# Centring a head's values as they are turned, before the recurrence, instead of centring its outputs

## The chip, the cores and the metric

One core of one Trainium2 chip. The metric is the device time of one execution in microseconds (us); lower is better. A core has a matrix engine (TensorE, PE in the rows, with its weight loads as PEld), a vector engine (VectorE, DVE), a scalar engine (ScalarE, ACT), GpSimd (POOL) and a queue that issues the transfers (SyncE, SP). PSUM is the memory into which TensorE writes, in banks of 128 x 512 float32.

## What is computed

A decoder trunk of two layers on one sequence of 512 tokens of width 1024. Every layer is a half-weighted SwiGLU block, a mixer, and another half-weighted SwiGLU block, each behind an RMS norm and added to the state. The mixer of layer 0 is an RWKV-7 recurrence over 12 heads of 64 channels, beside an attention to a memory of 256 tokens; that of layer 1 is a dilated window attention, beside the same kind of memory attention. What matters here is how the recurrence's output is normalized:

```
def step(state, inp):
    r_t, w_t, k_t, v_t, kk_t, a_t = inp
    sa = einsum('bhvk,bhk->bhv', state, -kk_t)
    state = state * w_t + sa[..., None] * (kk_t * a_t) + v_t[..., None] * k_t
    return state, einsum('bhvk,bhk->bhv', state, r_t)

y = rwkv7_scan(r_h, w_h, k_h, v_h, kk, a_h)
mean = jnp.mean(y, axis=-1, keepdims=True)
var = jnp.mean(jnp.square(y - mean), axis=-1, keepdims=True)
y = (y - mean) * lax.rsqrt(var + LNX_EPS) * lnx_g + lnx_b
bonus = jnp.sum(r_h * k_h * r_k, axis=-1, keepdims=True) * v_h
y = (y + bonus) * g
```

The state is linear in v, row by row of its v index, and so is the output. The mean of y over a head's 64 channels is therefore what the recurrence gives for the mean of v over these channels; with values whose mean over a head is zero, y has mean zero.

## The kernel before

Activations lie as channels x tokens: tiles of 128 channels and all 512 tokens. A dense product splits both operands in a high and a low float32r part and adds three matmuls of 128x512 (`dense`); ScalarE makes a weight tile's high part (`whi`), VectorE or GpSimd the low one (`wlo`), and SP fetches the weights (`raw`). Small products, those of the recurrence among them, are plain float32.

The mixer of layer 0 (`mixer_a`) works on 6 pairs of heads, 128 channels each, and in chunks of 64 tokens. For each pair:
- `projections` makes k, r and v with dense products.
- `rwkv_prepare` makes the decays, the normalized key, the operands `AR`, `beta`, `kappa` of the chunked form; it turns v from channels x tokens to tokens x channels (line 842, `turned`: four TensorE transposes into one bank, then ScalarE copies it to `vt`), and multiplies the bonus's head sum (`bon`, a matmul with the constant `other`) with the channels' own v into `bv`.
- `rwkv_solve` inverts each chunk's triangular system by doubling (`tx`, `TT`) and makes `WU` from it.
- `rwkv_finish` carries the state over the 8 chunks (`H`) into `py`; ScalarE copies `py` into `y0` in two halves (a `tmp` tile). Then the mean over a head comes from a matmul with the constant `same` (line 1048), VectorE subtracts it, ScalarE squares, `roots` sums the squares by head, takes reciprocal and root, `spread` brings the result back to channels x tokens with four matmuls against `ident`, and three VectorE steps apply gain, offset with `bv`, and gate.

The order is made in Python: `weave` steps through generators ("strands": finish, two solves, prepare, two memory attentions, projections, `first_pass`) by a clock that a `Meter` keeps from estimated durations, with the times of writes and reads under the tensor's name. A strand goes on when its clock has passed what it issued; the earlier one in the list goes first. `rwkv_prepare` of pair j waits until pair j-2 is finished, `projections` of pair j until pair j-2 is prepared. `first_pass` begins the output projection with five of the six pairs' outputs; the rest of it follows the weave.

Small tiles: `roots` (line 556) takes a 128x8 tile from the state's pool, with 12 buffers (`ROOTS`, line 227). With `wide` it is read once, by ScalarE's root; without, it stays as the norms of a query tile until the attention has used them. `warm` (line 382) runs a first ScalarE instruction on a tile of its own. The constants are one table that a single transfer loads (`load_constants`, line 387).

In the rows a bank is named by its kind (`sc`, `mm`, `py`, `fps`), a constant's slice is `cst`, and all instructions of the engines have line 295, that of the wrapper which notes their cost.

Of the kernel before, what the change touches and what calls it, by code (L numbers as in the profile page):

```python
# [10 lines left out]
F32 = mybir.dt.float32  # L11
F32R = mybir.dt.float32r
AF = mybir.ActivationFunctionType
ALU = mybir.AluOpType
# [3 lines left out]
P = 128  # L18
T = 512
# [4 lines left out]
HD = 64  # L24
NPAIR = 6
MEM = 256
C = 64
# [3 lines left out]
EPS = 1e-6  # L31
LNX_EPS = 64e-5
# [3 lines left out]
LEVELS = (2, 4, 8, 16)  # L36
Q = 32
# [4 lines left out]
def t5_buckets(dist):  # L42
    dist = np.maximum(np.asarray(dist), 0)
    large = 16 + (
        np.log(np.maximum(dist, 1).astype(np.float32) / np.float32(16.0))
        / np.float32(math.log(128.0))
        * np.float32(16.0)
    ).astype(np.int32)
    return np.where(dist < 16, dist, np.minimum(large, 31))


def constants():
    f = np.float32
    i = np.arange(P)
    same = (i[:, None] // HD == i[None, :] // HD).astype(f)
    ident = np.eye(P, dtype=f)
    cols = [ident, same, 1.0 - same, np.ones((P, P), f)]

    s, t = np.arange(C)[:, None], np.arange(C)[None, :]
    pairs = [s < t, s <= t, (s // 2 == t // 2) & (s % 2 == 0) & (t % 2 == 1)]  # L60
    pairs.append(s == t)
    cols += [np.concatenate([m.astype(f)] * 2, 0) for m in pairs]

    q, u = np.arange(Q)[:, None], np.arange(Q)[None, :]
    for b in LEVELS:
        cols.append(np.concatenate([((q // (2 * b) == u // (2 * b)) & (q // b % 2 == 1) & (u // b % 2 == 0)).astype(f)] * 4, 0))
    cols.append(np.concatenate([(q == u).astype(f)] * 4, 0))
    cols.append(np.repeat(i[:, None] // Q % 2 == np.arange(2)[None, :], Q, 1).astype(f))

    hot, neg = np.zeros((32, 9, 256), f), np.full((12, 9, 256), NEG, f)  # L70
    m = np.arange(255)
    diff = 127 - m
    for v in range(9):
        if v < 7:
            dist = (3 - v) + DIL * diff
            ok = (dist >= 0) & (dist <= 128)
        elif v == 7:
            dist, ok = DIL * diff, diff >= 0
        else:
            dist, ok = DIL * diff, (diff >= 0) & (diff % 4 == 0)  # L80
        hot[t5_buckets(dist)[ok], v, m[ok]] = 1.0
        neg[:, v, m[ok]] = 0.0
    return np.concatenate(cols, 1), hot.reshape(32, 9 * 256), neg.reshape(12, 9 * 256)


CONST_W = [P, P, P, P, 2 * C, C, C, *([Q] * len(LEVELS)), Q, 2 * Q]
CONST_N = ["ident", "same", "other", "ones", "mprod", "first", "stack", *[f"lvl{b}" for b in LEVELS], "square", "diagonal"]

# [11 lines left out]
def pack(x, mem, ffn_pre_norm, ffn_pre_w_in, ffn_pre_w_out, mix_norm, ffn_post_norm, ffn_post_w_in,  # L102
# [41 lines left out]
    at["lg"], at["lb"] = col(a_lnx_g[0][sw]), col(a_lnx_b[0][sw])  # L144
    a["vec"] = np.concatenate(vec, 0).T
    a["cst"], a["hot"], a["neg"] = constants()
    return {k: np.ascontiguousarray(v) for k, v in a.items()}, at

# [19 lines left out]
def wide(t):  # L168
    return t.unsqueeze(1).broadcast_to([P, NCH, C])
# [54 lines left out]
        return r  # L224


ROOTS = 12
WAIT, FREE = "wait", "free"


# [108 lines left out]
def until(test):  # L339
    if not test():  # L340
        yield test
# [7 lines left out]
class Net:  # L349
# [21 lines left out]
    def load_vectors(self):  # L371
        nc = self.nc
        self.vec = self.cp.tile(list(self.ap["vec"].shape), F32, name="vec")
        nc.sync.dma_start(self.vec, self.ap["vec"])
        self.eps = self.cp.tile([P, 1], F32, name="eps")
        nc.gpsimd.memset(self.eps, EPS)

        self.gains = self.cp.tile([P, 3], F32, name="gains")
        for i, (q, k) in enumerate(GAINS):
            nc.vector.tensor_scalar(self.gains[:, i:i + 1], self.v(q), self.v(k), 0.125, op0=ALU.mult, op1=ALU.mult)  # L380

    def warm(self):

        t = self.cp.tile([P, 1], F32, name="warm")
        self.nc.scalar.activation(t, self.eps, AF.Square)

    def load_constants(self):
        nc = self.nc
# [3 lines left out]
        off = 0  # L392
        for n, w in zip(CONST_N, CONST_W):
            setattr(self, n, t[:, off:off + w])
# [150 lines left out]
                nc.scalar.activation(vt[:, :, (j - 2) * P:(j - 1) * P], tp.rearrange("p (b u) -> p b u", u=P), AF.Copy)  # L545
                yield FREE

    def head_rms(self, t, n, tmp, bank, wide=False):


        sq = tmp()
        self.nc.scalar.activation(sq, t, AF.Square)
        yield WAIT
        return (yield from self.roots(sq, n, bank, tmp if wide else None, 1.0 / HD, EPS, ALU.mult, ALU.add))

    def roots(self, sq, n, bank, wide, *change):

        nc, nb = self.nc, n // P
        ps = bank("sc")[:, :nb * 2].rearrange("p (b e) -> p b e", e=2)
        for b in range(nb):  # L560
            nc.tensor.matmul(ps[:, b], sq[:, b * P:(b + 1) * P], self.pair, start=True, stop=True,
                             skip_group_check=True)
        r = self.xp.tile([P, 4, 2], F32, tag="roots", bufs=ROOTS, name=self.nm("roots"))[:, :nb]
        nc.vector.tensor_scalar(r, ps, *change[:2], **{f"op{i}": o for i, o in enumerate(change[2:])})
        nc.vector.reciprocal(r, r)
        yield WAIT
        if wide:
            w = wide().rearrange("p (b e u) -> p b e u", e=2, u=HD)
            nc.scalar.activation(w, r.unsqueeze(3).broadcast_to([P, nb, 2, HD]), AF.Sqrt)
            r = w.rearrange("p b e u -> p b (e u)")  # L570
        else:
            nc.scalar.activation(r, r, AF.Sqrt)
        yield WAIT
        return r
# [79 lines left out]
    def mixer_a(self, xin, u, kv, mid, nexts, dst, after):  # L654
        nc, tc = self.nc, self.tc
        w = self.ap["wa_in"]
        with ExitStack() as ctx:
# [23 lines left out]
            q, rr = [], []  # L681
# [46 lines left out]

            def memory(j):
                yield from until(lambda: len(q) > j)  # L730
                r = yield from self.head_rms(q[j], T, self.tmp, bank)
                yield from until(lambda: self.made[NPAIR - 1])
                yield from self.memory_attention(j, q[j], r, kv, pool, bank, om[j])

# [41 lines left out]
    def tmp(self):  # L776
        return self.big("tmp", self.tmps)
# [7 lines left out]
    def rwkv_prepare(self, j):  # L785

        nc = self.nc
        vec, gp, act, pe = nc.vector, nc.gpsimd, nc.scalar, nc.tensor
        col = {n: t[:, j:j + 1] for n, t in self.cols.items()}
        k, r, v = self.krv[j]  # L790
# [13 lines left out]
        sq = self.tmp()  # L804
# [7 lines left out]
        yield WAIT  # L812
        Ei = self.tmp()
        act.activation(Ei, L, AF.Exp, scale=-1.0)
        root = yield from self.roots(sq, T, self.bank, self.tmp, 1e-24, None, ALU.max)
        inv = self.bank("sc")
        self.spread(root, inv)
        kk = sq
# [20 lines left out]
        rk = b2  # L839
        vec.scalar_tensor_tensor(rk, r, self.v("rk", j), k2, op0=ALU.mult, op1=ALU.mult)  # L840
        yield WAIT
        ps = self.turned(lambda b: v[:, b * P:(b + 1) * P])
        vt = self.big("vt", 2, (P, 4, P))
        act.activation(vt, ps, AF.Copy)
        yield WAIT
# [131 lines left out]
    def rwkv_finish(self, j, y):  # L977

        nc = self.nc
        vec, gp, act, pe = nc.vector, nc.gpsimd, nc.scalar, nc.tensor  # L980
# [9 lines left out]
        with self.packed(4):  # L990
            for b, c, e in spots:
                pe.matmul(kg[c][own(e), 0, b], wu[own(c), e, b, :C], Mb[own(c), e, b, 1], start=b == 0, stop=False,
                          skip_group_check=True)
            for b, c, e in spots:
                if 0 < 2 * b + c < NCH - 1:
                    pe.matmul(kg[c][own(e), 1, b], wu[own(c), e, b, :C], tb[own(c), b, own(e)], start=False,
                              stop=b == 3, skip_group_check=True)
# [8 lines left out]
        with self.packed(4):  # L1006
            for b, c, e in spots:
                pe.matmul(py[c][own(1 - e), 0, b], wu[own(c), e, b, C:], Mb[own(c), e, b, 1], start=b == 0, stop=False,
                          skip_group_check=True)
            for b, c, e in spots:  # L1010
                pe.matmul(py[c][own(1 - e), 0, b], vt[own(c), b, own(1 - e)], Mk[own(c), e, b, 1], start=False,
                          stop=False, skip_group_check=True)

            for b, c, e in spots[::-1]:
                if 2 * b + c < NCH - 1:
                    pe.matmul(py[c][own(e), 1, b], tb[own(c), b, own(e)], wu[own(c), e, b, C:], start=False, stop=False,
                              skip_group_check=True)
                    pe.matmul(py[c][own(e), 1, b], tk[own(c), b, own(e)], vt[own(c), b, own(1 - e)], start=False,
                              stop=False, skip_group_check=True)
# [9 lines left out]
        for i in range(1, NCH):  # L1029
            b, c = divmod(i - 1, 2)  # L1030
            act.activation(H[:, i], py[c][:, 1, b], AF.Copy, scale=E[:, i - 1, C:])
            yield WAIT
            b, c = divmod(i, 2)
            with self.packed(4):
                if i > 1:
                    readout(i - 1)
                if i < NCH - 1:
                    for e in range(2):
                        pe.matmul(py[c][own(e), 1, b], G[own(e), c, b], H[own(e), i], start=False, stop=i >= NCH - 3,
                                  skip_group_check=True)  # L1040
# [3 lines left out]
        y0 = self.tmp()  # L1044
        for c in range(2):
            act.activation(y0.rearrange("p (b c u) -> p b c u", c=2, u=C)[:, :, c], py[c][:, 0], AF.Copy)
        yield WAIT
        mean = self.bank("sc")
        pe.matmul(mean, self.same, y0, start=True, stop=True)
        vec.scalar_tensor_tensor(y0, mean, -1.0 / HD, y0, op0=ALU.mult, op1=ALU.add)  # L1050
        sq = self.tmp()
        act.activation(sq, y0, AF.Square)
        yield WAIT
        root = yield from self.roots(sq, T, self.bank, self.tmp, 1.0 / HD, LNX_EPS, ALU.mult, ALU.add)
        var = self.bank("sc")
        self.spread(root, var)
        vec.scalar_tensor_tensor(y0, y0, self.v("lg", j), var, op0=ALU.mult, op1=ALU.mult)
# [50 lines left out]
    def mixer_b(self, xin, u, rkv, ukv, kv, bdram, mid, nexts, dst, after):  # L1108
        nc, tc = self.nc, self.tc
        wq, wkv = self.ap["wb_q"], self.ap["w_kv"]  # L1110
        with ExitStack() as ctx:
# [15 lines left out]
            q = [pool.tile([P, T], F32, name=self.nm("qn")) for _ in range(8)]  # L1127
            om = [pool.tile([P, T], F32, name=self.nm("yb")) for _ in range(4)]
            rr, rq = [], {}
# [25 lines left out]
            def settle():  # L1155
                n = 0
                while n < 20:
                    yield from until(lambda: later)
                    kind, m, t = later.pop(0)
                    n += 1  # L1160
                    if kind == "v":
                        yield WAIT
                        ps = self.turned(lambda b: t[:, b * P:(b + 1) * P])
                        nc.scalar.activation(vt[:, :, m * P:(m + 1) * P], ps, AF.Copy)
                        yield WAIT
                    elif kind == "k":
                        yield from self.head_norm(kh[:, m], t, self.gain(2), self.tmp, bank, T)
                    else:
                        rq[m] = yield from self.head_rms(t, T, self.tmp, bank)
                    done.add((kind, m))  # L1170

            def dilated(par):
# [170 lines left out]
```

## Time and profile before

| | |
|---|---|
| timed runs, median of 3 | 2123.32 us (2123.22 to 2123.34) |
| the profiled execution | 2117.79 us |
| its span | 2116.0 us |
| granted TensorE clock, mean | 0.995 of full |
| TensorE busy | 2068.4 us |
| VectorE, ScalarE, GpSimd busy | 872.1, 813.3, 587.7 us |

The span runs from the first to the last instruction of the profiled execution. A row of a timeline has an instruction's start, its duration, engine, line, operation, output and inputs with their shapes, a count where equal ones are merged, and in brackets how long the engine was idle before it and what ended that. Ends of matmuls are modelled, since they are pipelined: the distance between starts is the firmer number.

### The profile page before, as it was taken

To read this page: it belongs to the slowest core of one execution; us is meant where nothing else is said; L and a number is where in the kernel's file an instruction comes from. 1 tells how busy PE (TensorE), PEld (TensorE's weight loads), DVE (VectorE), ACT (ScalarE), POOL (GpSimd) and SP (SyncE) were. 2 spreads that over 40 slices of the span, in tenths; PEclk is the share of its full clock that TensorE was granted. 3 is DMA by queue.
4 is the path that set the end of the run, shared out by engine and by line. 5 is a ranking of instruction groups with operands and counts; after the bars stand their busy time and mean duration, and the time that the engine had idled before them with its cause. 6 is when DMAs were issued, how large, how long until landed. Compare 5 with 4: busy or idle time off the path is not lost. (4 is left out here: it accounts for less than half of the span.)

```text
span 2116.0 us, 35895 instructions
## 1 busy us (share of the span) xinstructions
PE 2068.4 (98%) x14582; PEld 1662.6 (79%) x14582; DVE 872.1 (41%) x1300; ACT 813.3 (38%) x1416; POOL 587.7 (28%) x513
## 2 busy tenths in 40 slices
PE   8999999989999999999999999999999999999999
PEld 6888888867677677788888888888787768888887
DVE  6333333454555455333433533333326375333322
ACT  6333333433334544333433433333336554333321
POOL 2222222553332152222222222222232224222221
PEclk9999999999999999999999999999999999999999
DMA  5332344411110173443344433334431154333342
GB/s 195 100 95 95 95 123 131 122 47 35 35 33 26 36 249 114 131 150 98 108 134 126 148 95 100 95 102 124 145 103 51 41 165 159 95 96 99 102 123 80
DMA packets 130645, 222.07 MB, mean 105 GB/s; under 512 B 14232, under 2 KB 31824, under 8 KB 130480
## 3 DMA queue, kind: packets, MB, share of 16 engines
q1 hardware_dynamic: 130480, 219.78, 34.0%
q8 instruction: 114, 1.87, 0.4%
q14 instruction: 51, 0.42, 0.1%
HBM read 202.84 MB, written 21.61 MB: 106 GB/s over the span
## 5 line engine op out<-in xcount | busy, mean ns | idle before, releaser
L295 POOL TENSOR_TENSOR wlo<-raw,whi 128x512 fp32r<-128x512 f32 (+3 forms) x404 | 494.5, 1225 | 1422.7 <-ACT whi L295 1412.2
L295 ACT ACTIVATE whi<-raw 128x512 fp32r<-128x512 f32 (+3 forms) x684 | 416.2, 610 | 938.9 <-PE fps L295 792.3
L295 PE MATMUL fps<-uh,whi 128*128 128x512 f32 x1408 | 551.6, 392 | 7.6 <-ACT whi L295 7.6
L295 PE MATMUL fps<-uh,wlo 128*128 128x512 f32 x1408 | 549.7, 390 | 2.1 <-POOL wlo L295 1.8
L295 PE MATMUL fps<-ul,whi 128*128 128x512 f32 x1408 | 548.9, 390 | 0.0
L295 DVE TENSOR_TENSOR wlo<-raw,whi 128x512 fp32r<-128x512 f32 x280 | 201.8, 721 | 355.4 <-ACT whi L295 346.4
L295 PEld LDWEIGHTS fps<-uh,whi 128*128 128x128 f32 x1408 | 264.8, 188 | 67.7 <-ACT whi L295 11.2
L295 PEld LDWEIGHTS fps<-uh,wlo 128*128 128x128 f32 x1408 | 264.8, 188 | 60.2 <-POOL wlo L295 3.9
L295 PEld LDWEIGHTS fps<-ul,whi 128*128 128x128 f32 x1408 | 264.9, 188 | 55.8 <-issue 0.7
L295 PE MATMUL fps<-hh,wlo 128*128 128x512 f32 x704 | 278.1, 395 | 0.0
L295 PE MATMUL fps<-hh,whi 128*128 128x512 f32 x704 | 278.1, 395 | 0.0
L295 PE MATMUL fps<-hl,whi 128*128 128x512 f32 x704 | 278.1, 395 | 0.0
L295 DVE TENSOR_TENSOR gs<-fps,rstd 128x512 f32<-128x512 f32 x88 | 60.5, 690 | 322.9 <-PE fps L295 322.9
L295 PEld LDWEIGHTS fps<-hh,wlo 128*128 128x128 f32 x704 | 132.2, 188 | 32.2
L295 PEld LDWEIGHTS fps<-hl,whi 128*128 128x128 f32 x704 | 132.2, 188 | 32.1
L295 PEld LDWEIGHTS fps<-hh,whi 128*128 128x128 f32 x704 | 132.2, 188 | 31.9
L295 PE MATMUL mm<-uh,whi 128*128 128x512 f32 x280 | 123.0, 439 | 1.0 <-DVE x L295 0.7
L295 PE MATMUL mm<-ul,whi 128*128 128x512 f32 x280 | 113.2, 404 | 0.0
L295 PE MATMUL mm<-uh,wlo 128*128 128x512 f32 x280 | 112.3, 401 | 0.0
L295 DVE TENSOR_TENSOR hm<-fps,gs 128x512 f32<-128x512 f32 x88 | 60.6, 691 | 121.2 <-PE fps L295 115.4
L295 DVE TENSOR_TENSOR hl<-hm,hh 128x512 fp32r<-128x512 f32 x88 | 77.2, 880 | 51.1 <-ACT hh L295 51.0
L295 PEld LDWEIGHTS mm<-uh,whi 128*128 128x128 f32 x280 | 53.2, 190 | 17.5 <-issue 4.6
(259 smaller groups left out, 2044.0 us busy)
## 6 DMA issues: line engine op xcount, KB each, us to landing
raw<-w SPq DMA_DIRECT2D x512, 256.0 KB, 2.6
raw<-wa_in SPq DMA_DIRECT2D x44, 256.0 KB, 2.7
xd<-x SPq DMA_DIRECT2D x40, 256.0 KB, 2.9
tmp<-xd SPq DMA_DIRECT2D x32, 256.0 KB, 3.2
xin<-xd SPq DMA_DIRECT2D x32, 256.0 KB, 4.3
raw<-w_kv SPq DMA_DIRECT2D x24, 256.0 KB, 2.6
raw<-w SPq DMA_DIRECT2D x32, 128.0 KB, 2.2
raw<-wmem SPq DMA_DIRECT2D x16, 256.0 KB, 2.6
```

The source lines that it names most:

```text
L295: r = f(*args, **kw)
```

## The change

The table of constants gets a fifth 128x128 block, `center`, which is the identity less 1/64 within a head. In `rwkv_prepare` the four transposes of v become four float32 matmuls with v's block as the stationary operand and `center` as the moving one, so that the turned values come out with their head's mean removed; the bonus still uses the channels' own v. In `rwkv_finish` the mean's matmul and its subtraction are gone. Besides, the norms of the eight query tiles get a fixed tile `query_roots` in the constants' pool, the other norms two buffers there, and `warm` writes a fourth column of `gains` instead of a tile of its own.

```
-    cols = [ident, same, 1.0 - same, np.ones((P, P), f)]
+    cols = [ident, same, 1.0 - same, np.ones((P, P), f), ident - same / HD]
...
-ROOTS = 12
...
-        self.gains = self.cp.tile([P, 3], F32, name="gains")
+        self.gains = self.cp.tile([P, 4], F32, name="gains")
+        self.query_roots = self.cp.tile([P, 8, 4, 2], F32, name="qroots")
...
-        t = self.cp.tile([P, 1], F32, name="warm")
-        self.nc.scalar.activation(t, self.eps, AF.Square)
+        self.nc.scalar.activation(self.gains[:, 3:], self.eps, AF.Square)
...
-        r = self.xp.tile([P, 4, 2], F32, tag="roots", bufs=ROOTS, name=self.nm("roots"))[:, :nb]
+        r = keep or self.cp.tile([P, 4, 2], F32, tag="roots", bufs=2, name=self.nm("roots"))[:, :nb]
...
-                r = yield from self.head_rms(q[j], T, self.tmp, bank)
+                r = yield from self.head_rms(q[j], T, self.tmp, bank, keep=self.query_roots[:, j])
...
-        ps = self.turned(lambda b: v[:, b * P:(b + 1) * P])
+
+        ps = self.bank("sc", (P, 4, P))
+        for b in range(4):
+            pe.matmul(ps[:, b], v[:, b * P:(b + 1) * P], self.center, start=True, stop=True, skip_group_check=True)
         vt = self.big("vt", 2, (P, 4, P))
         act.activation(vt, ps, AF.Copy)
...
-        mean = self.bank("sc")
-        pe.matmul(mean, self.same, y0, start=True, stop=True)
-        vec.scalar_tensor_tensor(y0, mean, -1.0 / HD, y0, op0=ALU.mult, op1=ALU.add)
         sq = self.tmp()
         act.activation(sq, y0, AF.Square)
...
-                        rq[m] = yield from self.head_rms(t, T, self.tmp, bank)
+                        rq[m] = yield from self.head_rms(t, T, self.tmp, bank, keep=self.query_roots[:, m])
```

## Rows read from the trace of the kernel before

**Rows 1.** The page, part 1: busy us, share of the span, instructions.

```profile
PE 2068.4 (98%) x14582; PEld 1662.6 (79%) x14582; DVE 872.1 (41%) x1300; ACT 813.3 (38%) x1416; POOL 587.7 (28%) x513
```

**Rows 2.** Busy time by stretch: length, PE, PEld, DVE, ACT, POOL, clock, DMA.

```profile
395.00:761.00 366.00, 339.18 (x6676) 258.22 (x6675) 187.31 (x335) 146.00 (x286) 139.55 (x142) 0.98 0.17 51
...
1530.00:1760.00 230.00, 223.63 (x1281) 175.45 (x1282) 113.20 (x209) 118.40 (x233) 75.66 (x63) 0.99 0.34 106
```

**Rows 3.** TensorE's waits, 395 to 785 us: total us, times, longest.

```profile
PE sc L295 <- DVE tx L295: 12.8, 8, 2.9
```

**Rows 4.** Timelines of ScalarE and VectorE: a split of `y`, the fifth `y`.

```profile
665.41 0.61 ACT L295 ACTIVATE uh<-y 128x512 fp32r<-128x512 f32 x1
...
721.69 0.69 DVE L295 TENSOR_TENSOR y<-sc,tmp 128x512 f32<-128x512 f32 x1 [0.20 <-PE sc L295]
```

**Rows 5.** Busy time by stretch, after the last pair is finished.

```profile
748.00:761.00 13.00, 12.80 (x57) 10.27 (x57) 3.76 (x7) 4.43 (x9) 5.01 (x6) 1.00 0.83 264
```

**Rows 6.** TensorE's timeline, pair 5: mean, dense work, `spread`, the gate's matmul.

```profile
739.57 1.04 PE L295 MATMUL sc<-tmp,cst 128*128 128x512 f32 x2
...
740.68 0.40 PE L295 MATMUL mm<-uh,whi 128*128 128x512 f32 x1
740.92 0.39 PE L295 MATMUL mm<-ul,whi 128*128 128x512 f32 x1
...
744.45 1.05 PE L295 MATMUL sc<-cst,tmp 128*128 128x128 f32 x8
745.34 1.02 PE L295 MATMUL sc<-gl,lora 128*128 128x512 f32 x2
```

**Rows 7.** VectorE's timeline, pair 5: the mean's subtraction.

```profile
740.65 0.69 DVE L295 SCALAR_TENSOR_TENSOR tmp<-sc,tmp 128x512 f32<-128x512 f32 x1 [8.94 <-PE sc L295]
```

**Rows 8.** TensorE's timeline, pair 0: the turn of v, the bonus matmul.

```profile
431.23 0.60 PE L295 MATMUL sc<-cst,krv 128*128 128x128 f32 x4
431.58 0.48 PE L295 MATMUL mm<-uh,whi 128*128 128x512 f32 x1
...
435.59 1.13 PE L295 MATMUL sc<-tmp,cst 128*128 128x512 f32 x2 [2.37 <-DVE tmp L295]
```

**Rows 9.** ScalarE's timeline, pairs 0 and 5: copies out of `py`, the square.

```profile
496.71 0.66 ACT L295 ACTIVATE tmp<-py 128x256 f32<-128x256 f32 x2 [1.50 <-PE py L295]
500.67 0.63 ACT L295 ACTIVATE tmp<-tmp 128x512 f32<-128x512 f32 x1 [1.14 <-DVE tmp L295]
...
738.77 0.66 ACT L295 ACTIVATE tmp<-py 128x256 f32<-128x256 f32 x2 [0.59 <-PE py L295]
...
741.37 0.63 ACT L295 ACTIVATE tmp<-tmp 128x512 f32<-128x512 f32 x1 [1.94 <-DVE tmp L295]
```

**Rows 10.** The head, 0 to 25 us: the constants' transfer (us to landing), ScalarE's timeline.

```profile
cst<-cst SPq DMA_DIRECT2D x1, 496.0 KB, 7.2
...
2.03 0.20 ACT L295 ACTIVATE warm<-eps 128x1 f32<-128x1 f32 x1
4.34 0.72 ACT L295 ACTIVATE uh<-x,vec 128x512 fp32r<-128x512 f32 x1 [2.12 <-DMA x<-xT]
...
14.82 2.18 ACT L295 ACTIVATE whi<-raw 128x512 fp32r<-128x512 f32 x4
```

**Rows 11.** TensorE's timeline: the long hole and a small one, before the solve's matmuls.

```profile
468.64 1.06 PE L295 MATMUL sc<-tx,mb 32*32 32x32 f32 x32 [2.93 <-DVE tx L295]
...
545.19 0.74 PE L295 MATMUL sc<-tx,mb 32*32 32x32 f32 x64 [1.84 <-DVE tx L295]
```

**Rows 12.** Busy time by stretch at the two holes; the clock is third from the end.

```profile
465.00:480.00 15.00, 12.07 (x124) 9.05 (x124) 6.40 (x9) 3.28 (x7) 5.64 (x6) 0.66 0.10 33
545.00:550.00 5.00, 4.81 (x143) 3.90 (x144) 1.34 (x4) 0.66 (x2) 0.00 (x0) 0.67 0.01 3
```

More of the change, by code (lines that the diff above doesn't have):

```diff
@@ L83, in constants @@
     return np.concatenate(cols, 1), hot.reshape(32, 9 * 256), neg.reshape(12, 9 * 256)
-CONST_W = [P, P, P, P, 2 * C, C, C, *([Q] * len(LEVELS)), Q, 2 * Q]
-CONST_N = ["ident", "same", "other", "ones", "mprod", "first", "stack", *[f"lvl{b}" for b in LEVELS], "square", "diagonal"]
+CONST_W = [P, P, P, P, P, 2 * C, C, C, *([Q] * len(LEVELS)), Q, 2 * Q]
+CONST_N = ["ident", "same", "other", "ones", "center", "mprod", "first", "stack", *[f"lvl{b}" for b in LEVELS], "square", "diagonal"]
 def tiles_of(w):
@@ L546, in memory_kv, with head_rms @@
                 yield FREE
-    def head_rms(self, t, n, tmp, bank, wide=False):
+    def head_rms(self, t, n, tmp, bank, wide=False, keep=None):
         sq = tmp()
@@ L553, in head_rms, with roots @@
         yield WAIT
-        return (yield from self.roots(sq, n, bank, tmp if wide else None, 1.0 / HD, EPS, ALU.mult, ALU.add))
-    def roots(self, sq, n, bank, wide, *change):
+        return (yield from self.roots(sq, n, bank, tmp if wide else None, keep, 1.0 / HD, EPS, ALU.mult,
+                                      ALU.add))
+    def roots(self, sq, n, bank, wide, keep, *change):
         nc, nb = self.nc, n // P
@@ L814, in rwkv_prepare @@
         act.activation(Ei, L, AF.Exp, scale=-1.0)
-        root = yield from self.roots(sq, T, self.bank, self.tmp, 1e-24, None, ALU.max)
+        root = yield from self.roots(sq, T, self.bank, self.tmp, None, 1e-24, None, ALU.max)
         inv = self.bank("sc")
@@ L1053, in rwkv_finish @@
         yield WAIT
-        root = yield from self.roots(sq, T, self.bank, self.tmp, 1.0 / HD, LNX_EPS, ALU.mult, ALU.add)
+        root = yield from self.roots(sq, T, self.bank, self.tmp, None, 1.0 / HD, LNX_EPS, ALU.mult, ALU.add)
         var = self.bank("sc")
```

## The prediction, made before the changed kernel had run

> **What bounds the kernel now.** I read the page first, then the busy time by stage, then TensorE's waits in the stage that the change touches, then the timelines around the changed lines. On the page TensorE is busy for 98% of the span [rows 1]: what is taken from another engine is worth nothing unless TensorE waits for it. By stage, TensorE is busy for 339.18 of the 366 us of the first mixer (395 to 761 us) [rows 2]. So this mixer, where the whole recurrence runs, has 27 us of idle TensorE. Who ends it: 12.8 us ends with VectorE's `tx`, the tiles of the triangular inverse in the solve [rows 3]. The mean and its subtraction are not behind these: the longest of the eight (2.93 us, at 468.64) comes before pair 0's outputs are copied at all, at 496.71 [rows 9, 11].
>
> The order on an engine is not only the one that `weave` writes. `first_pass` asks for five finished outputs, yet ScalarE splits the first of them at 665.41, while the fifth is written only at 721.69 [rows 4]. So instructions whose data are there move up past later ones, and the dense work of the output projection fills holes that the recurrence leaves. The recurrence's last matmul starts at 745.34 [rows 6], and from 748 to 761 dense work still fills 12.80 of the 13 us [rows 5]. Hence my reading: not the recurrence's chain sets the end of the stage, but TensorE's work plus its idle time. A shorter chain lets dense work move to earlier places, and is paid for only as far as TensorE's work shrinks or its holes close.
>
> **The change part by part.** *The mean's matmul* (128x512, float32, two records). The records' durations are modelled ends, so I take starts. In pair 5 the mean starts at 739.57 and the second dense matmul behind it at 740.68, 1.11 us later; one dense matmul starts 0.24 us after the one before it (740.68 to 740.92) [rows 6]. The mean takes 1.11 - 0.24 = 0.87 us. Six times: **-5.2 us** of TensorE.
>
> *Its subtraction*, 0.69 us of VectorE in each of 6 pairs [rows 7], 4.1 us in all, lies beside TensorE's work. I count nothing; if that cover were gone it would be worth up to 0.69 us a pair.
>
> *The turn of v*: now four transposes, one record each; afterwards four matmuls against `center`. In pair 0 the four start at 431.23 and the next work at 431.58: 0.35 us [rows 8]. The new form isn't in the trace under these names, but `spread` runs the same shape: float32, 128x128 stationary, 128x128 moving, two records a block, four blocks. It takes from 744.45 to 745.34, 0.89 us [rows 6]. The bounds are 0.87 (the mean: as many columns in one piece) and 1.05 (the group's modelled end) [rows 6]; it can't fall below a transpose's 0.35, having twice the records. I take 0.89, the same shape. So 0.54 us more per pair, six times: **+3.2 us**; by the bounds +3.1 to +4.2.
>
> The Trainium skill ("TensorE: Matmul & The Clock Gate", section Terms) calls the transpose mode 4 times faster for FP32. The rows give 0.89 against 0.35, a factor of 2.5. By the skill's factor the six turns would cost 6.3 us more (6 x 1.05), and the sum below would be +0.3 instead of -2.3.
>
> *Where the turn's addition falls*: pair 0's stands ahead of the bonus matmul, which starts at 435.59 after 2.37 us of idle TensorE, waiting for VectorE's `tmp`, the product of r, k and their weight [rows 8]. VectorE's chain to it doesn't pass the turn, so this one addition is swallowed: **-0.5 us**. I credit no such hole behind the other five turns. The bonus matmul is queued behind the turn, and VectorE's `bv` behind that, so `made` comes 0.5 us later, for which `rwkv_solve` waits. ScalarE's copy of the turned block keeps its shape.
>
> *The wait that goes*: after its two copies out of `py` ScalarE waits for mean and subtraction before it squares. In pair 0 the copies end at 497.37 (496.71 + 0.66) and the square starts at 500.67: 3.3 us. In pair 5 it is 739.43 to 741.37: 1.9 us [rows 9]. The square will follow the copies on its own engine; what is late next are the head sums of `roots`, in order on TensorE. By the reading above this latency is worth nothing where dense work is at hand; the first rival takes the other view.
>
> *Constants*: the table grows by 128 columns, 64 KB on 496 KB, which land after 7.2 us [rows 10]. In proportion that is 64/496 x 7.2 = 0.9 us more at most, and not below 0. On SP the weights of the next two column tiles are queued behind it, and share its DMA engines. But ScalarE reaches these weights only at 14.82, straight from a square, with no wait before them [rows 10]. I take **+0.2 us**, nearer to 0 than to 0.9.
>
> *Small tiles.* `warm` now writes a column of `gains`, beside the three that VectorE writes. It runs at 2.03, and ScalarE's first real work is at 4.34, when x is there [rows 10]: a wait for VectorE's columns would have some 2 us of room. Two buffers of `roots` instead of twelve: only the wide users (`rwkv_prepare`, `rwkv_finish`, the k norms) take them, and each releases its own as soon as ScalarE's root has read it. At most two strands use them at a time, so 0. The planner keeps its times under a tensor's name, so the eight query roots in one tile look to it as if they waited for each other's readers. That can move orders in the second mixer, where TensorE is idle for 230 - 223.63 = 6.4 us [rows 2]. From nothing to one hole like the 1.84 us one of the solve [rows 11], either way; I take 0 and keep the bounds for the range.
>
> **Sum**: -5.2 + 3.2 - 0.5 + 0.2 = **-2.3 us**. Against the profiled execution, 2117.79 (span 2116.0, 1.8 us around it), that is 2115.5, and a span of 2113.7. The median of the timed runs is 2123.32, 5.5 us above the profiled one; I carry the difference over: **2121.0 us**, 0.11% less. About 0.2%, 4.2 us, is what a measurement of this kernel can tell from no change, so this counts as the same.
>
> **The rivals.**
> *The chain counts (faster).* `rwkv_prepare` of pair j waits for `rwkv_finish` of j-2, `rwkv_solve` for the first, `rwkv_finish` for the second: two loops of three pairs each. The idle time in the solves shows that fill is not always at hand. The waits that go are 3.3 and 1.9 us in the first and the last pair [rows 9], 2.6 in the mean, 15.6 for six. With two loops side by side half of it shows, 7.8, less half of the six later `made` (6 x 0.54 / 2 = 1.6): -6.2, **2117.1**. Against it: in pair 5 dense work starts right behind the mean, at 740.68 and before [rows 6]. Chance 0.22.
>
> *The long hole goes (faster).* Before 468.64 TensorE is idle for 2.93 us [rows 11]. From 465 to 480 the granted clock is 0.66 in the mean [rows 12], which is 10 us at the 1.2 GHz level, and costs 15 x 0.34 = 5.1 us at most. The planner's clock is moved by the first turn already, 37 us earlier. If the order there comes out without the hole: -2.3 - 2.9 - 5.1 = -10.3, **2113.0**. Chance 0.12.
>
> *Another such hole (slower).* The same place the other way: every order after the first turn is drawn up anew, and work that waits can end up ahead of a `tx` on VectorE that TensorE needs. A small one, as before 545.19: 1.84 us of idle [rows 11] and a clock of 0.67 over the next 5 us, 1.7 us [rows 12]: +3.5, net +1.2, **2124.5**, still the same. One like the long one: +8.0, net +5.7, **2129.0**. It decides once new idle and slow time is 6.5 us above the old. For it: this order too is planned from estimated durations, and has two such holes. Against it: VectorE has 4.1 us less in its queue. Chance 0.16 for a long one or several small ones, 0.06 for a single small one.
>
> *The turn costs four times what it costs now.* That is 4 x 0.35 = 1.40 us, 1.05 more a pair, of which pair 0's is swallowed by its 2.37 us hole: 5 x 1.05 - 5.2 + 0.2 = +0.3, **2123.6**. `spread`'s 0.89 speaks against it. Chance 0.04. The Trainium skill's rule named above would give this.
>
> **How the numbers follow.** The forecast (a gain of 0 to 4 us) has 0.40; the chain 0.22; the hole gone 0.12; new holes 0.16 and 0.06; the dear turn 0.04. Faster by over 0.2% (under 2119.1): the chain, the hole gone, and 0.02 of the forecast's own edge, 0.36. Slower (over 2127.6): 0.16. The rest, 0.48, is within. The range takes in the chain, a small hole and the bounds of the unknown costs (the turn's +1.0, the table's +0.7, the second mixer's 1.84 either way), and reaches to the hole gone; beyond it lie the long new holes: 2113 to 2127. The likeliest case alone: 2119 to 2123.5.
>
> **What would show it.** The mean's records are gone, and each turn has eight records and takes about 0.9 us by its starts. TensorE's busy time in the first mixer falls by 2 to 3 us; the square follows the copies out of `py` at once. If the stage ends more than 4 us earlier while the turn takes its 0.9 us, the chain counted, or a hole went: TensorE's idle time in the stage (27 us now) and the slow stretches of its clock tell which. If it ends later, the same two tell where. If time goes or comes after 785 us, my zero for the small tiles is wrong, and with it the forecast.

## The result, and the profile after

The changed kernel takes 2110.09 us in the median (2109.29 to 2115.47, 6 runs) against 2123.33 (2123.22 to 2123.56): a ratio of 0.9943 [0.993, 0.9956], 13.2 us less. That is 10.9 us below the forecast and 2.9 below the range. The profiled execution shows less of it, 2113.38 us (span 2111.6) against 2117.79 (span 2116.0), and its clock was granted at 0.989 in the mean, against 0.995 before.

Where the time went is read from the first and last `fps` matmul of the four SwiGLU blocks (their starts in TensorE's timeline; `fps` are the banks of these blocks alone). In brackets stands what was lost to the clock inside the first mixer: half of the time in which only the 1.2 GHz level was granted.

| us | before | after | difference |
|---|---|---|---|
| first block | 382.1 | 380.2 | -1.9 |
| first mixer (of it lost to the clock) | 389.7 (8.5) | 395.0 (15.4) | +5.3 |
| second and third block | 747.8 | 739.2 | -8.6 |
| second mixer | 221.2 | 225.4 | +4.2 |
| fourth block | 364.2 | 360.6 | -3.6 |

So the gain lies in the four blocks, which the change doesn't mention, and both mixers, which it does, are longer in this execution. Page part 1, the stretches and TensorE's waits in the first mixer, for [rows 1 to 3]:

```profile
PE 2061.6 (98%) x14594; PEld 1670.4 (79%) x14594; DVE 867.3 (41%) x1294; ACT 817.3 (39%) x1418; POOL 590.7 (28%) x513
```

```profile
395.00:761.00 366.00, 337.60 (x6664) 259.46 (x6664) 182.73 (x328) 147.68 (x285) 136.58 (x139) 0.96 0.16 49
1530.00:1760.00 230.00, 222.86 (x1269) 174.24 (x1269) 111.26 (x207) 115.86 (x229) 75.87 (x62) 0.98 0.31 99
```

```profile
PE sc L294 <- DVE tx L294: 14.0, 11, 3.0
...
PE sc L294 <- DVE tmp L294: 1.9, 1, 1.9
```

TensorE is as full as before, the longest waits are of the old kind, and in the first mixer the share of the clock fell from 0.98 to 0.96. What differs in the blocks shows in the groups of matmuls by shape over the whole span: count, busy us, mean ns. First before, then after; `uh` are the operands of the first products, `hh` and `hl` those of the second.

```profile
L295 PE MATMUL fps<-uh,wlo 128*128 128x512 f32 x1408 | 549.7, 390 | 2.1 <-POOL wlo L295 1.8 <-DVE wlo L295 0.3
...
L295 PE MATMUL fps<-hh,wlo 128*128 128x512 f32 x704 | 278.1, 395 | 0.0
```

```profile
L294 PE MATMUL fps<-uh,wlo 128*128 128x512 f32 x1408 | 550.5, 391 | 0.6 <-POOL wlo L294 0.6
...
L294 PE MATMUL fps<-hh,wlo 128*128 128x512 f32 x704 | 273.9, 389 | 0.0
```

The same instruction with the same shape took 395 ns in the second products before, and 389 after; in the first products it stayed. Ends are modelled, so here are starts, in the fourth block, before and after:

```profile
2049.72 0.40 PE L295 MATMUL fps<-hh,whi 128*128 128x512 f32 x1
2049.96 0.39 PE L295 MATMUL fps<-hl,whi 128*128 128x512 f32 x1
2050.19 0.40 PE L295 MATMUL fps<-hh,wlo 128*128 128x512 f32 x1
2050.43 0.39 PE L295 MATMUL fps<-hh,whi 128*128 128x512 f32 x1
```

```profile
2049.82 0.39 PE L294 MATMUL fps<-hh,whi 128*128 128x512 f32 x1
2050.04 0.39 PE L294 MATMUL fps<-hl,whi 128*128 128x512 f32 x1
2050.27 0.39 PE L294 MATMUL fps<-hh,wlo 128*128 128x512 f32 x1
2050.50 0.39 PE L294 MATMUL fps<-hh,whi 128*128 128x512 f32 x1
```

Three matmuls take 0.71 us before and 0.68 after. Over all neighbours in the trace, without the few with a wait between them, the second products start 233.3 ns apart before and 226.7 after, the first ones 226.8 in both. 704 x 3 = 2112 matmuls by 6.6 ns are 13.9 us; the keys' and values' product of the second mixer (288 matmuls, some 232 to 229 ns) gives about 1 more.

Their order, their waits and their data are the same. What differs is where the tiles lie in a partition's memory. By the addresses in the built programs the operands `hh` of the second products lie 384 bytes off the weights' tiles before (counted modulo 2048, the size of a tile row), and 0 after; `uh` 0 in both. The small tiles did this: the constants' pool lies ahead of the weights, the state's pool behind them. With `roots` out of the state's pool, 12 x 32 = 384 bytes between weights and `hh` are gone.

### The profile page after: what moved, and what is told of

It reads as the page before. It is cut to its first block, busy times and chain, and to the rows that moved or that the text cites. A ratio compares the mean times of both kernels' runs of the same rounds, so it can differ in the third digit from the quotient of the medians.

```text
span 2111.6 us, 35927 instructions
## 1 busy us (share of the span) xinstructions
PE 2061.6 (98%) x14594; PEld 1670.4 (79%) x14594; DVE 867.3 (41%) x1294; ACT 817.3 (39%) x1418; POOL 590.7 (28%) x513
## 4 chain that ended last, share of the span: by engine, by line
PE 65%; DVE 1%; ACT 0%; issue 0%; POOL 0%; ACTq 0%; POOLq 0%; DVEq 0%
PE fps L294 52%; PE mm L294 7%; PE sc L294 5%; PE py L294 1%; DVE prob L294 0%; DVE x L294 0%; DVE mpr L294 0%; ACT krv L294 0%; DVE mx L294 0%; POOL wlo L294 0%; DVE dmx L294 0%; ACT mpr L294 0%; DVE tmp L294 0%; ACT L294 0%; DVE krv L294 0%
```

## The experiments

Ratios are against the kernel before on the same chip; it had medians of 2123.17 beside the first four kernels from tiles_only to roots24, 2123.29 beside the three with "apart" in their name, and 2121.24 beside roots20, turn_alone and mean_gone. So kernels of different sets are compared by their difference to the kernel before in their own. "Distance" is from the weights to `hh`, in bytes modulo 256; "ns" is the mean distance of starts in the second products; the mixers go from `fps` to `fps` as above, of the one profiled execution.

| kernel | distance | ns | median us | ratio | first mixer (clock) | second mixer |
|---|---|---|---|---|---|---|
| before | 128 | 233.3 | 2123.33 | | 389.7 (8.5) | 221.2 |
| after | 0 | 226.7 | 2110.09 | 0.9943 [0.993, 0.9956] | 395.0 (15.4) | 225.4 |
| tiles_only | 0 | 226.6 | 2110.42 | 0.9947 [0.9934, 0.9961] | 390.4 (8.5) | 223.9 |
| after_state_roots | 64 | 228.9 | 2108.45 | 0.994 [0.9926, 0.9954] | 389.0 (10.2) | 223.1 |
| roots16 | 0 | 226.6 | 2104.44 | 0.9911 [0.9898, 0.9925] | 388.7 (6.8) | 220.3 |
| roots24 | 0 | 226.7 | 2105.88 | 0.9922 [0.991, 0.9935] | 393.9 (11.9) | 220.0 |
| roots20 | 128 | 233.3 | 2120.52 | 1.0 [0.9991, 1.001] | 391.3 (8.5) | 221.0 |
| tiles_apart | 0 | 226.7 | 2107.35 | 0.9927 [0.9915, 0.994] | 393.0 (13.7) | 220.4 |
| center_apart | 0 | 226.7 | 2105.93 | 0.993 [0.991, 0.9951] | 393.7 (13.7) | 219.9 |
| center_apart128 | 128 | 233.3 | 2117.21 | 0.9977 [0.9968, 0.9986] | 389.8 (10.2) | 220.9 |
| turn_alone | 0 | 226.7 | 2109.38 | 0.9941 [0.9926, 0.9955] | 396.8 (11.9) | 220.0 |
| mean_gone | 0 | 226.7 | 2099.38 | 0.9894 [0.9879, 0.9908] | 387.2 (13.7) | 220.1 |

**The small tiles without the centring (tiles_only).** The kernel before with the diff's edits of the small tiles (`gains`, `query_roots`, `warm`, `roots`), but neither `center` nor the new turn, and with the mean as it was.

```
-        r = self.xp.tile([P, 4, 2], F32, tag="roots", bufs=ROOTS, ...
+        r = keep or self.cp.tile([P, 4, 2], F32, tag="roots", bufs=2, ...
```

> The kernel before with the small tiles moved as in the change (query norms in a fixed tile, two buffers for the others, both in the constants' pool), without the centring. Theory A, places in memory: the 384 bytes of the norms' twelve buffers no longer stand between the weights and the FFN's hidden tiles hh and hl, so these start at the same place within 512 bytes as the weight tiles; dense matmuls on hh, hl start every 226.6 ns as on uh, ul, and not every 233.3. 2112 of them times 6.6 ns is 13.9 us, and 288 on kvh, kvl some 1.4 more: 2108 us. Theory B, the centring shortens the chain of the recurrence: without it nothing is gained, hh stays at 233 ns, 2123 us.

2110.42, 12.7 us under the kernel before on the same chip: the small tiles, costed at zero in the prediction, give nearly the whole gain.

**The change with two small tiles put back (after_state_roots).**

```
-        r = keep or self.cp.tile([P, 4, 2], F32, tag="roots", bufs=2, ...
+        r = keep or self.xp.tile([P, 4, 2], F32, tag="roots", bufs=2, ...
```

> The changed kernel with the two buffers of roots back in the state's pool, 64 bytes between the weights and what lies behind the state; the order of all instructions is that of the changed kernel. Theory A: hh and hl are at 233 ns again, and the time is the kernel before's less what the centring is worth by itself: 2121 to 2125 us. Theory B: as fast as the changed kernel, 2110 us.

A miss for places in memory as I had put it: two tiles are 64 bytes, and the pace is 228.9 ns, not 233. Some distances are nearly as good as 0, so not every shift counts. At that pace it should still be 4.6 us (2112 x 2.2 ns) slower than the changed kernel, and it is 1.6 faster; its runs had a mean clock of 0.993 against 0.991, and the intervals are some 3 us either way, so the median says nothing about 64 bytes.

**The kernel before with other numbers of buffers (roots16, roots24, roots20).** One number, `ROOTS = 12`, becomes 16, 24, 20. The instructions and their order are those of the kernel before on every engine; only what lies behind moves, by 128, 384 and 256 bytes.

> The kernel before with sixteen buffers of roots instead of twelve: 512 bytes instead of 384 between weights and hidden tiles; the order of all instructions is that of the kernel before. Theory A with a period of 512 bytes: hh, hl and kvh, kvl at 226.6 ns, 2108 us. Theory A with a period of 1024 or 2048 bytes (only the very same place counts): 233 ns, 2123 us. Theory B: 2123 us.

> The kernel before with twenty-four buffers of roots: 768 bytes between weights and hidden tiles, that is 256 within 512; the order is that of the kernel before. Theory A with a period of 256 bytes: 226.6 ns, 2108 us. Theory A with a period of 512 or more: 233 ns, 2123 us. Theory B: 2123 us.

> The kernel before with 20 buffers of small tiles instead of 12: the same instructions in the same order, the moving tiles of the second products 128 bytes off the weights (mod 256). With 16 buffers (distance 0) it was 2104.4, with 24 (distance 0) 2105.9. Theory 'distance': the second products run at 233.3 ns as in the row of matmuls measured alone, so 2119 to 2123, as the kernel before. Rival 'buffers': more buffers for the small tiles were what helped; then 2104 to 2106, between 16 and 24.

16 and 24 buffers give 2104.44 and 2105.88, 20 gives 2120.52 and a ratio of 1.0. More buffers are not the cause, since 20 lies between; the distance is. The groups by shape from 1800 to 2090 us, of 16 and of 20 buffers:

```profile
L295 PE MATMUL fps<-uh,wlo 128*128 128x512 f32 x261 | 101.5, 389 | 0.0
L295 PE MATMUL fps<-hh,wlo 128*128 128x512 f32 x166 | 64.6, 389 | 0.0
```

```profile
L295 PE MATMUL fps<-uh,wlo 128*128 128x512 f32 x283 | 110.1, 389 | 0.0
L295 PE MATMUL fps<-hh,wlo 128*128 128x512 f32 x140 | 55.3, 395 | 0.0
```

**The pace by itself (pace).** Rows of 48 dense matmuls out of one tile:

```
for name, (w, m, n) in zip(NAMES, plan):
    ...
    c, t = w // 4 + i % 4 * P, 704 + m // 4
    nc.tensor.matmul(ps, both[:, c:c + P], both[:, t:t + T], ...)
```

> Only a row of dense float32r matmuls (128x128 stationary, 128x512 moving) out of one tile, no other engine at work beside them; the rest of the computation is left out. The first block of 96 is to raise the clock; then 48 matmuls for each distance of the moving tile from a base that lies a multiple of 256 bytes from the stationary tiles: 0, 32, ... 512, then 640, 768, 896, 1024 bytes; then both moved together and the stationary ones alone, by 32, 64, 128 and 256 bytes; then 0 and 384 twice in turn. Theory 'distance': 226.7 ns a matmul where the distance is a multiple of 256 bytes (0, 256, 512, 768, 1024), 233.4 ns at 128, 384, 640, 896 and most others, 64 in between; the stationary ones moved alone by 32, 64 or 128 give the slow pace, both moved together the fast one; 0 and 384 in turn repeat it. Rival 'address': the pace hangs on the moving tile's own address, so both moved together by 128 is as slow as the moving one alone, and the stationary ones alone make no difference. Rival 'company': the slower pace comes from what other engines do at the same time (weights being split, transfers), so here every block has the same pace.

TensorE's timeline; a line is one row, and its pace is the distance to the start of the next line, by 48. `ob` to `of` have the distances 0, 32, 64, 96 and 128, `oj` has 256; in `ow` the stationary tiles alone are moved by 32, in `ox` both.

```profile
33.97 11.04 PE L35 MATMUL ob<-both 128*128 128x512 f32 x48
44.85 11.37 PE L35 MATMUL oc<-both 128*128 128x512 f32 x48
56.05 11.16 PE L35 MATMUL od<-both 128*128 128x512 f32 x48
67.05 11.37 PE L35 MATMUL oe<-both 128*128 128x512 f32 x48
78.26 11.36 PE L35 MATMUL of<-both 128*128 128x512 f32 x48
89.46 11.40 PE L35 MATMUL og<-both 128*128 128x512 f32 x48
...
123.08 11.05 PE L35 MATMUL oj<-both 128*128 128x512 f32 x48
133.97 11.37 PE L35 MATMUL ok<-both 128*128 128x512 f32 x48
...
267.27 11.36 PE L35 MATMUL ow<-both 128*128 128x512 f32 x48
278.46 11.06 PE L35 MATMUL ox<-both 128*128 128x512 f32 x48
289.36 11.36 PE L35 MATMUL oy<-both 128*128 128x512 f32 x48
```

0: 10.88 us by 48 is 226.7 ns. 32: 11.20, 233.3. 64: 11.00, 229.2. 96 and 128: 233.5 and 233.3. 256: 226.9. Stationary tiles alone moved: 233.1; both: 227.1. The other rows fit: 226.9 to 227.1 at 512, 768 and 1024, 229.2 at 320, 233 to 234 at the rest, 384 among them, but for the stationary tiles alone moved by 128, with 232.1. With ScalarE's copy of each finished bank as the only other work, company is out; with both moved and the pace unchanged, the address alone is out. The distance modulo 256 decides.

**Which stationary tile counts (pace_next).** The same rows with four stationary places in turn, `place = (0, 32, 128, 160)`, and the moving tile at the place of the k-th one on.

> Again only rows of 48 dense matmuls out of one tile; the rest of the computation is left out. Which stationary tile counts: a matmul's own, or one that is loaded while it streams? Four stationary tiles in turn lie at 0, 32, 128 and 160 bytes (mod 256), so that any two of them are at a slow distance from each other. In the row 'own' the moving tile has the place (mod 256) of its own stationary tile, in 'next' that of the following matmul's, in 'second' that of the one after it, in 'third' that of the fourth, which is also the one before. Each row twice; rows at 0 throughout and at 128 throughout stand before and behind. If what costs is the load of the next stationary tile beside the moving tile's stream: 226.7 ns in the row 'next', 233.3 in the other three. If a matmul's own pair counts: 226.7 in 'own' alone. If the load runs two ahead: 226.7 in 'second' alone.

Two rows of controls (0 and 128), then own, next, second, third, and own again:

```profile
34.31 11.04 PE L37 MATMUL ob<-both 128*128 128x512 f32 x48
45.19 11.35 PE L37 MATMUL oc<-both 128*128 128x512 f32 x48
56.38 11.43 PE L37 MATMUL od<-both 128*128 128x512 f32 x48
67.65 11.29 PE L37 MATMUL oe<-both 128*128 128x512 f32 x48
78.77 11.57 PE L37 MATMUL of<-both 128*128 128x512 f32 x48
90.18 11.37 PE L37 MATMUL og<-both 128*128 128x512 f32 x48
101.38 11.29 PE L37 MATMUL oh<-both 128*128 128x512 f32 x48
112.50 11.28 PE L37 MATMUL oi<-both 128*128 128x512 f32 x48
```

The controls give 226.7 and 233.1 ns, own 234.8 (231.7 the second time), next 231.7, second 237.7, third 233.3. No row reaches 226.7: a miss for all three theories. So what collides, and when, stays open; shown is only that the distance costs.

**The name of the query tiles (tiles_apart, center_apart).** Eight tiles instead of one, without and with the centring:

```
-        self.query_roots = self.cp.tile([P, 8, 4, 2], F32, name="qroots")
+        self.query_roots = [self.cp.tile([P, 4, 2], F32, name=self.nm("qroots")) for j in range(8)]
```

> The kernel before with the small tiles moved as in the change (no centring), but the eight query tiles' norms are eight tiles with names of their own instead of one. Every engine has the same instructions in the same order as before; the moving tiles of the second products lie at a distance of 0 from the weights (mod 256 bytes). The runs so far: 2110.4 with one tile for all eight, 2104.4 with the kernel before and four more small tiles. Theory 'names': the one name makes the planner put the second mixer in another order, which costs about 3 to 6 us; with names of their own 2104 to 2106, and the second mixer back at 239 us from 242.5. Rival 'no order': the second mixer's 3 us are chance of the single profiles, and this is 2109 to 2111 like the one with one tile.

> The whole change, but with eight tiles with names of their own for the query tiles' norms. The second mixer's order is that of the kernel before; the first mixer has the change's order; distance 0. Against the run with the same small tiles and no centring this is the centring alone. By the sum of the prediction the centring is worth -2.3: 2.3 under that run, so about 2102 if that one is at 2104.4. Theory 'names': 2100 to 2104, 6 to 8 under the changed kernel. Rival 'chain counts': 6 or more under the run without centring, 2098. Rival 'no order': at the changed kernel's 2110.

With one name the second mixer takes 223.9 us (tiles_only) and 225.4 (after), with eight 220.4 and 219.9, and against their own kernel before they are 3.2 and 4.1 us better (-15.9 against -12.7, and -17.4 against -13.2). (The 239 and 242.5 us of the expectation run between other marks, from one norm's reciprocal to the next.) With one name TensorE waits for VectorE's `mpr`; with eight this wait is down to 0.3. The waits of the second mixer (1515 to 1770 us) in tiles_only, then in tiles_apart:

```profile
PE sc L294 <- DVE mpr L294: 1.7, 2, 0.9
```

```profile
PE sc L294 <- ACT mpr L294: 0.3, 1, 0.3
```

This is near the width of the intervals, some 3 us either way, but it comes twice, and the stage shows it each time. Of the stage's 3.5 and 5.5 us, 1.7 and 3.4 were lost to the clock, which was at its lower level for longer in these two profiles with one name; 1.8 and 2.1 us remain. after_state_roots, with one name too, lost no more to it than the kernels with eight, and takes 223.1. tiles_apart came out 1.4 above what was expected, and center_apart 1.4 under it, where 2.3 was forecast for the centring.

**The change at the old distance (center_apart128).** As center_apart, with four of the eight small tiles in the state's pool behind `uh` and `ul`.

```
+        self.query_roots += [self.xp.tile([P, 4, 2], F32, name=self.nm("qroots")) for j in range(4)]
```

> As the run before it, with four of the eight small tiles moved behind the operand tiles in the state's pool: the same instructions in the same order on every engine, but the moving tiles of the second products (and of the keys' and values' product) lie 128 bytes off the weights (mod 256), as they did in the kernel before; the first products keep their distance of 0. Theory 'distance': 2112 + 288 matmuls at 6 to 6.7 ns, so 13 to 16 us more than the run before it, 2114 to 2119; 233 ns from start to start in the second products. Rival 'chance': the two are within 3 us.

The same instructions in the same order, 128 bytes apart: 11.3 us more in the median, 233.3 ns again. The median is where it was expected, though the difference is 1.7 us under the lower end that the count gave; in its profile the first mixer lost 3.5 us less to the clock than center_apart's.

**The two halves of the centring (turn_alone, mean_gone).** center_apart with the mean's matmul and subtraction put back, and center_apart with the four transposes put back, so that nothing is centred in it.

```
+        mean = self.bank("sc")
+        pe.matmul(mean, self.same, y0, start=True, stop=True)
+        vec.scalar_tensor_tensor(y0, mean, -1.0 / HD, y0, op0=ALU.mult, op1=ALU.add)
```

```
-            pe.matmul(ps[:, b], v[:, b * P:(b + 1) * P], self.center, ...
+        ps = self.turned(lambda b: v[:, b * P:(b + 1) * P])
```

> The change with eight small tiles of their own (distance 0, the second mixer's order that of before), but the mean's matmul and its subtraction are left in: v is turned by the four matmuls against center, and the outputs, whose mean is zero by then, are centred again. Against the same without any centring (2107.4, 2106 to 2109 by its runs). By the prediction's terms: six turns at 0.46 to 0.54 us more, one of them swallowed, +2.3 to +2.7, so about 2110. By the turn at four times its price: +5.2, 2112.5. Rival 'order': the first mixer's time hangs on how its work comes to lie and on the clock, and no term of this size shows, 2107 or less.

> The same small tiles, v turned by the four transposes as in the kernel before, and the mean's matmul and subtraction gone: the outputs are not centred at all, that part is left out. The order is that of the whole change but for two places in the first mixer. By the prediction's terms: 5.2 us under the run without centring (2107.4), so 2102, and 2.3 to 2.7 under the whole change with the same small tiles (2105.9). Rival 'chain counts': the shorter chain is paid for on top, 2098 or less. Rival 'order': no difference to the whole change beyond 1 us.

The differences to the kernel before are -11.9 (turn_alone), -21.9 (mean_gone), -15.9 (tiles_apart, neither half) and -17.4 (center_apart, both). Taking the mean away gives -5.9 and -5.5 us, as it is done beside the transposes or beside the new turn; the turn costs 4.1 and 4.5, and both together -1.4. With intervals of some 3 us either way, 4 for center_apart, a single one of these differences is near its noise; the two of each kind together bear out the sign, and the sizes stay rough. The first mixer, what the clock cost taken off, has the same signs: 384.9 us with the turn alone, 373.5 with the mean gone, 379.3 to 382.8 with neither, 378.8 to 380.0 with both.

The turn itself, in pair 0 of mean_gone and of center_apart, with the dense matmul behind it:

```profile
428.89 0.60 PE L294 MATMUL sc<-cst,krv 128*128 128x128 f32 x4
429.25 0.48 PE L294 MATMUL mm<-uh,whi 128*128 128x512 f32 x1
```

```profile
428.16 1.05 PE L294 MATMUL sc<-cst,krv 128*128 128x128 f32 x8
428.96 0.48 PE L294 MATMUL mm<-uh,whi 128*128 128x512 f32 x1
```

0.36 against 0.80 us. But for two places these kernels have the same order on TensorE, so their starts can be laid side by side. What the clock took taken off, the distance grows by some 0.5 us at each turn, 3 us in six, and by about as much again between the turns, where the solves lie.

## Why the prediction was wrong

**The step that failed** is "Small tiles", and in it "At most two strands use them at a time, so 0". It asked who waits for a buffer and what the planner believes. Both questions were right, and the second had a real answer: one name costs 3 to 4 us in the medians, some 2 in the stage without what the clock took, where I had bounded it by 1.84. What it never asked is where the other tiles lie once the small ones are moved. The account of the 13.2 us: -15.9 for the places (tiles_apart; 13.9 and about 1 of it are counted in the trace), +3.2 for the one name (tiles_only against tiles_apart), and -0.5 for the centring (after against tiles_only). roots16 and roots24 show 18.7 and 17.3 for the places, and the interval of roots16, 15.9 to 21.7, doesn't reach down to the counted 14.9. Much of what is above is the clock: their runs were granted 0.995 and 0.993 in the mean, the kernel before beside them 0.992. Of 107 runs whose clock is on record, one that had 0.001 less than the mean of its kernel took some 1.4 us longer. Set to equal clocks by this estimate, roots16, roots24 and tiles_apart gain 13.8, 15.2 and 15.1 us, which is what the count gives.

The view was at hand: the page of the kernel before lists the first and the second products with 390 and 395 ns for the same instruction and shape. I read the page for what is dear and for idle time, and there two groups without idle time looked settled. The prediction's own last sentence held, though: time went after 785 us, and the zero for the small tiles was the reason.

**What bounds the kernel** held. TensorE is at 98% as before, and a matmul that is shorter by 3% was paid out in full.

**The mean's matmul**, -5.2, held as far as the intervals tell: -5.5 and -5.9 in the medians, its subtraction included. **The turn**, 0.89 by `spread`'s shape, held as a price of its own: 0.81 in pair 0 of the changed kernel, the start at 429.46 to that at 430.27, and 0.91 in the four pairs behind it.

```profile
429.46 1.05 PE L294 MATMUL sc<-cst,krv 128*128 128x128 f32 x8
430.27 0.48 PE L294 MATMUL mm<-uh,whi 128*128 128x512 f32 x1
...
433.81 1.35 PE L294 MATMUL sc<-tmp,cst 128*128 128x512 f32 x2 [1.92 <-DVE tmp L294]
```

Against the 0.35 us of [rows 8] that is a factor of 2.3, so the rival of the turn at four times its price is out, and the factor 4 of the Trainium skill ("TensorE: Matmul & The Clock Gate", section Terms) doesn't hold for these blocks. **The swallowed addition** is in the last line: the hole before the bonus matmul shrank from 2.37 to 1.92 us, by about the 0.46 that the turn grew. Yet the six turns together cost 4.1 to 4.5 us in the medians, more than the 3 of their own starts; the holes of the solves behind them, which I credited with nothing, may be where the rest went.

**The wait that goes**, for [rows 9], ScalarE's timeline in pairs 0 and 5: the square follows the copies with no gap.

```profile
496.01 0.66 ACT L294 ACTIVATE tmp<-py 128x256 f32<-128x256 f32 x2 [1.50 <-PE py L294]
496.70 0.63 ACT L294 ACTIVATE tmp<-tmp 128x512 f32<-128x512 f32 x1
...
744.14 0.66 ACT L294 ACTIVATE tmp<-py 128x256 f32<-128x256 f32 x2 [0.59 <-PE py L294]
744.83 0.63 ACT L294 ACTIVATE tmp<-tmp 128x512 f32<-128x512 f32 x1
```

Whether this chain counted is not settled. With what the clock cost taken off, the first mixer takes 381.5 us in the mean of the six kernels that have mean and transposes, and 379.5 in the four with the change: -2.0, where the sum had -2.5. But the single ones of the six lie between 379.3 and 382.8, and at the old distance the whole change gave 6.1 us (3.0 to 6.8 by the interval), which the chain's rival would have given too (-6.2). Set to equal clocks as above, the centring is worth 2.1 us (after against tiles_only), 4.5 (center_apart against tiles_apart) and 4.9 (center_apart128 against before), at or above the sum's 2.3 and under the rival's 6.2.

**The constants**, +0.2: the table lands after 6.8 us against 7.2, and the first split of the weights starts at 15.78, for [rows 10]:

```profile
cst<-cst SPq DMA_DIRECT2D x1, 560.0 KB, 6.8
```

```profile
15.78 2.18 ACT L294 ACTIVATE whi<-raw 128x512 fp32r<-128x512 f32 x4
```

That split is 0.96 us later than in [rows 10], but with the old table it starts at 15.46 and 16.10 in roots16 and roots20, so no cost of the table shows.

**The holes** of [rows 11, 12] are still there, 2.96 and 1.86 us of idle, with the clock at 0.77 and 0.78, so the rival in which the long one goes is out.

```profile
468.62 1.02 PE L294 MATMUL sc<-tx,mb 32*32 32x32 f32 x32 [2.96 <-DVE tx L294]
```

```profile
543.20 0.75 PE L294 MATMUL sc<-tx,mb 32*32 32x32 f32 x64 [1.86 <-DVE tx L294]
```

```profile
465.00:480.00 15.00, 12.04 (x143) 9.29 (x144) 7.06 (x9) 3.72 (x7) 5.95 (x7) 0.77 0.09 30
545.00:550.00 5.00, 5.00 (x90) 3.97 (x89) 1.56 (x3) 1.92 (x4) 0.69 (x1) 0.78 0.01 3
```

The rival of new holes isn't: in this execution the clock took 6.9 us more of the first mixer than before, in stretches at other places too, and TensorE's idle time in it rose from 26.8 to 28.4 us. Together that is more than the 6.5 at which the prediction let this rival decide, and the places hid it. Over all kernels, though, what the clock took there goes from 6.8 to 13.7 us without the centring and from 10.2 to 15.4 with it. Whether the centring makes it worse can't be told from one profile each.

Several versions come out under both kernels, lowest among those that compute everything the kernel before with 16 or 24 small tiles instead of 12 (2104.44, 2105.88) and the change with eight small tiles of their own (2105.93); these can't be told apart.

## What to carry to other kernels

Before an edit of a small tile is costed at nothing, work out which tiles lie behind it and by how many bytes they move against the tiles that they are multiplied with. And compare the starts of equal instructions between groups that should be alike: a difference of 1 to 3% in a group of some thousand is worth more than most waits, and it shows in no list of waits. To learn what a change of a few us is worth, hold the places still, as center_apart128 and roots20 do.

## What the runs showed of the hardware

A dense float32r matmul of 128x512 that follows another one starts 226.7 ns behind it where moving and stationary tile lie a multiple of 256 bytes apart, 229.2 at 64, and 232 to 234 at the other multiples of 32 that were tried, 192 among them. The granted clock was 1.00 in all these rows, the 2.4 GHz level, and beside them ScalarE only copied a bank out once a row.

The Trainium skill ("SBUF — State Buffer", section "Who interferes with whom") gives TensorE two read ports, one for the moving operand and one for the load of the stationary one, that are independent, and says that TensorE never waits for anyone. The rows of the pace differ: with the same instructions TensorE loses 6.6 ns a matmul, 3%, by where its own two operands lie. By that page, as I read it, the pace would be one number at every distance, and the small tiles worth nothing, as I had them.
